# The recurrence of a state-space mixer from twenty steps to eighteen, with four pieces per chunk in separate steps, beside the projections of a decoder layer

## The chip, the core and the metric

The kernel runs on one core of a Trainium2 chip. The metric is the device time of one execution in microseconds (us). The engines are named as the profile names them: PE (TensorE, matrix products and transposes), DVE (VectorE), ACT (ScalarE), POOL (GpSimd) and SP (SyncE, which issues most loads).

## The reference

One decoder layer over 2048 tokens of width 1024, in float32. Its first part, in which the change lies, is a norm, one input projection, and two groups of heads side by side; the second group is the Mamba-2 recurrence in chunks of 128 tokens (12 heads of width 64, 4 groups of B and C, state 128):

```python
h = rmsnorm(x, mix_norm_w)
proj = h @ w_in                       # u (256) | z (768) | x, B, C (768 + 512 + 512) | dt (12)
y_s5 = s5_mixer(proj[..., :256], ...) # the diagonal group
# the recurrence (ssd_mixer): xs, bmat, cmat = silu(causal convolution of width 4)
xdt  = x * dt[..., None]
lmat = exp(where(causal, a_cs[l] - a_cs[s], -inf))        # decay in a chunk
cb   = einsum('bclgn,bcsgn->bcgls', cm, bm)
y_diag = einsum('bcgls,bcghls,bcsghp->bclghp', cb, lmat, xdt)
states = einsum('bclgn,bcghl,bclghp->bcghpn', bm, exp(a_cs[-1] - a_cs), xdt)
def step(carry, inp):                                     # over the 16 chunks
    st, dec = inp
    return carry * dec + st, carry
y = y_diag + einsum(cm, prev, exp(a_cs)) + x * d_skip
y_ssd = rmsnorm(y * silu(z), norm_w)
x = x + concatenate([y_s5, y_ssd]) @ w_out
```

Cross-attention into 256 memory tokens, a gated MLP with a convolution of width 3 and a last norm follow; the change does not touch them.

## The kernel before

Products run as three matmuls on pairs of a rounded value and its rest (`mm3`, L124 to L129): high by high, high by rest, rest by high. So each operand is split (`halves`): ACT writes the rounded half (L102 for weights, L105 for the normed input h), DVE the rest (L103, L106).

The mixer stage (`MixerIn.run`) takes the 2048 tokens in four blocks b of 512, each block in two halves pr of six heads. A block has 22 projections: two of u for the diagonal group, and in each half three of z, three of x, then B, C, B, C. Each projection (`proj`) is two parts of twelve matmuls 128x512; after each part it calls `k.step()`. The outputs of x, B and C go through the width-4 convolution (`conv`): the accumulation bank is read by ACT (L312, L315), the three taps are DVE's (L317), ACT takes the tanh (L319), and DVE's L320 writes the result. The last projection of each half is the second C. Between its last matmul and its L320 lies this whole sequence.

`k.step()` advances three lists of generators by one yield each: fg (the recurrence), bg (the norm of later tokens, the sum of squares `ssq`, the preparation of the memory) and xg (`s5_setup`, the diagonal group's setup, a separate stream that is appended at block 0, half 1; its table operations for POOL are L775 to L783 and its sums of products on DVE L699 to L701). When a half's projections have been issued, its recurrence `ssd(b, pr)` is put on fg and its steps lie between the parts of the projections that follow: those of half 0 in the twenty parts of half 1, those of half 1 in two steps at the next block's start and then in that block's u projections and half 0. At a block's start the eight inputs h of the next block are split with high priority, and their buffers come free when the last projection of the old block has read them. `k.drain()` issues at once what is left at a half's end.

The recurrence has these pieces for each chunk c:

- `decay(c)`: six exponentials on ACT (L407) in a tile of a ring of four that `fetch_L` filled earlier, by a DMA of POOL's queue (L391) and a masking on POOL (L392).
- `stage_in(c)`: three transposes of x (L419) that DVE scales by dt (L421) and by the decay (L422), and two of B (L425) that ACT copies (L427).
- `stage_cb(c)`: two products of B and C (L434), multiplied by the decay on DVE (L438, twice).
- `stage_y(c)`: the products with the old state (L447), the new state (L453) and the chunk itself (L461), with DVE's L449, L455, L456 and L462.
- `stage_out(c)`: three transposes (L470), then DVE's L473 and L474 for each.

After chunk 3 come the squares (ACT's L500, L503, DVE's L504), the scaling by the norm's weight (L505) and three output DMAs on ACT's queue (L506). When half 1 has ended, `ssq` is put on bg: four small matmuls (L517) of the summed squares `sqa`, two steps later.

Before the change the recurrence has twenty yields: `decay(0)`; then `head(0)`, which is `stage_in`, `stage_cb`, the next fetch and the next decay in one step; then for each chunk an empty step, `stage_y(c)`, an empty step, and `head(c+1)` with `stage_out(c-1)` in one step; then `stage_out(3)` and the squares.

A list scheduler orders each engine's queue from the order of issue and the priorities; the engines then work their queues in order and wait for each other by semaphores. Accumulation banks come from one pool of eight (`ps`), the recurrence's small tiles from a pool of fourteen (`u`).

Of the kernel before, what the change touches and what calls it, by code (L numbers as in the profile page):

```python
# [177 lines left out]
class MixerIn:  # L178
# [216 lines left out]
    def ssd(self, b, pr, dd, xs, Bs, Cs, zs, sqacc):  # L395
# [6 lines left out]
        def decay(c):  # L402

            L = Ls[c] = self.L.pop((b, pr, c))
            for hh in range(6):
                h = c * 12 + pr * 6 + hh
                S.activation(L[:, hh, :], L[:, hh, :], AF.Exp, bias=dd["nacs"][:, h:h + 1])  # L407
# [7 lines left out]
        def stage_in(c):  # L415
            cs = slice(c * 128, c * 128 + 128)
            px = k.ps()
            for i in range(3):
                TE.transpose(px[:, i * 128:i * 128 + 128], xs[i][:, cs], k.ident)  # L419
            xdt, xdd = self.u(), self.u()  # L420
            V.tensor_tensor(r6(xdt), r6(px[:, 0:384]), v6(dd["dt"], c), op=ALU.mult)  # L421
            V.tensor_tensor(r6(xdd), r6(xdt), Ls[c][:, :, 127:128].to_broadcast([P, 6, 64]), op=ALU.mult)  # L422
            pB = k.ps()
            for i in range(2):
                TE.transpose(pB[:, i * 128:i * 128 + 128], Bs[i][:, cs], k.ident)  # L425
            Bt = self.u(256)
            S.activation(Bt, pB[:, 0:256], AF.Copy)  # L427
            st[c] = [xdt, xdd, Bt]

        def stage_cb(c):  # L430
            cs = slice(c * 128, c * 128 + 128)
            pc = k.ps()
            for i in range(2):
                TE.matmul(pc[:, i * 128:i * 128 + 128], Bs[i][:, cs], Cs[i][:, cs], start=True, stop=True)  # L434
            M = [self.u() for _ in range(2)]
            for i in range(2):
                m3 = M[i].rearrange("p (h l) -> p h l", h=3)
                V.tensor_tensor(m3, Ls[c][:, i * 3:i * 3 + 3, :], pc[:, i * 128:i * 128 + 128].rearrange("p (h l) -> p h l", h=1).to_broadcast([P, 3, P]), op=ALU.mult)  # L438
            st[c].append(M)

        def stage_y(c):
            cs = slice(c * 128, c * 128 + 128)
            xdt, xdd, Bt, M = st[c]
            po = k.ps()
            for i in range(2):
                o = slice(i * 192, i * 192 + 192)
                TE.matmul(po[:, o], Cs[i][:, cs], self.prev[pr][:, o], start=True, stop=True)  # L447
            yo = self.u()
            V.tensor_tensor(r6(yo), r6(po[:, 0:384]), v6(dd["E"], c), op=ALU.mult)  # L449
            pS = k.ps()  # L450
            for i in range(2):
                o = slice(i * 192, i * 192 + 192)
                TE.matmul(pS[:, o], Bt[:, i * 128:i * 128 + 128], xdd[:, o], start=True, stop=True)  # L453
            np_ = self.u()
            V.tensor_tensor(r6(np_), r6(self.prev[pr]), v6(dd["cd"], c), op=ALU.mult)  # L455
            V.tensor_tensor(np_, pS[:, 0:384], np_, op=ALU.add)  # L456
            self.prev[pr] = np_
            pd = k.ps()
            for h in range(6):
                o = slice(h * 64, h * 64 + 64)  # L460
                TE.matmul(pd[:, o], M[h // 3][:, (h % 3) * 128:(h % 3) * 128 + 128], xdt[:, o], start=True, stop=True)  # L461
            V.tensor_tensor(yo, pd[:, 0:384], yo, op=ALU.add)  # L462
            st[c] = yo

        def stage_out(c):
            cs = slice(c * 128, c * 128 + 128)
            yo = st.pop(c)
            py = k.ps()
            for i in range(3):
                TE.transpose(py[:, i * 128:i * 128 + 128], yo[:, i * 128:i * 128 + 128], k.ident)  # L470
            for i in range(3):
                j = pr * 3 + i
                V.scalar_tensor_tensor(gt[i][:, cs], xs[i][:, cs], self.D[:, j:j + 1], py[:, i * 128:i * 128 + 128], op0=ALU.mult, op1=ALU.add)  # L473
                V.tensor_tensor(gt[i][:, cs], gt[i][:, cs], zs[j][:, cs], op=ALU.mult)  # L474
        def head(c):
            stage_in(c)
            stage_cb(c)
            n = pr * 4 + c + 3
            if n < 8:
                self.fetch_L(b, n // 4, n % 4)  # L480
            if c < 3:
                decay(c + 1)
        head(0)
        yield
        for c in range(4):
            yield
            stage_y(c)
            yield
            yield
            if c < 3:  # L490
                head(c + 1)
            if c:
                stage_out(c - 1)
            yield
        stage_out(3)
        yield
        for i in range(3):
# [1112 lines left out]
```

## Time and profile before

| what | us |
|---|---|
| three runs | 2756.7, 2758.6, 2751.95 |
| their median | 2756.7 |
| profiled execution | 2759.75 |
| its span | 2757.3 |
| PE busy | 2645.7 (96% of the span) |
| DVE busy | 2152.6 (78%) |
| ACT busy | 1326.6 (48%) |
| POOL busy | 495.9 (18%) |
| mean clock that PE was granted | 0.979 |

Durations below are from the one profiled execution, whose time lies 2.45 us over its span and 3.05 us over the median. In rows of a timeline the columns are start, duration, engine, line, operation, output and inputs, shape and count, and in brackets the idle time before it with what ended it. A matmul's duration covers its passage through the array, and matmuls overlap; the distance of starts tells their rate.

### The profile page before, as it was taken

Reading aid. Unit: us, or ns where it says so; the run is one execution under the profiler, and the core shown is the slowest. Engines: PE = TensorE matmul, PEld = TensorE weight load, DVE = VectorE, ACT = ScalarE, POOL = GpSimd, SP = SyncE. Lnnn points to the kernel's source line nnn. Section 1 sums busy time; section 2 is a strip of 40 time slices with the busy share of each in tenths; the row PEclk is TensorE's granted clock in tenths of the full one; section 3 lists DMA queues with packets and bytes.
Section 4 is the critical chain, followed back from the end, with each engine's and each line's share of the span. In section 5 each row is a group of like instructions: output and inputs, shape, how many; then the busy total and the mean of one; then the engine's idle time right before and its main releaser. Section 6 shows DMA issues by size and latency. Waiting matters only on the chain. (4 is left out here: it accounts for less than half of the span.)

```text
span 2757.3 us, 38540 instructions
## 1 busy us (share of the span) xinstructions
PE 2645.7 (96%) x12636; PEld 2199.3 (80%) x12636; DVE 2152.6 (78%) x4015; ACT 1326.6 (48%) x2657; POOL 495.9 (18%) x807
## 2 busy tenths in 40 slices
PE   8989988979999999999999999999999999999988
PEld 6768767857898788888888888887888888888876
DVE  8687788877887754878779788888887877677776
ACT  4654544435555612688745455445443444433333
POOL 1111144542002210110221222211211111000000
PEclk9989989979999999999999999999999999999999
DMA  6455333333259692645665343425322217887886
GB/s 197 154 174 156 123 126 108 117 114 111 92 180 296 236 331 102 230 153 206 210 233 196 116 133 111 133 85 168 103 74 92 84 62 235 287 291 244 261 267 202
DMA packets 241536, 468.22 MB, mean 170 GB/s; under 512 B 30008, under 2 KB 72056, under 8 KB 241336
## 3 DMA queue, kind: packets, MB, share of 16 engines
q1 hardware_dynamic: 182312, 341.38, 36.9%
q0 software_dynamic: 30416, 105.50, 11.8%
q10 hardware_dynamic: 28608, 18.88, 2.2%
q8 instruction: 100, 1.64, 0.2%
q14 instruction: 100, 0.82, 0.1%
HBM read 350.67 MB, written 114.39 MB: 169 GB/s over the span
## 5 line engine op out<-in xcount | busy, mean ns | idle before, releaser
L127 PE MATMUL ps<-H,W 128*128 128x512 f32 x952 | 370.7, 389 | 0.0
L128 PE MATMUL ps<-H,W 128*128 128x512 f32 x952 | 370.5, 389 | 0.2 <-DVE H L103 0.2
L129 PE MATMUL ps<-H,W 128*128 128x512 f32 x952 | 370.5, 389 | 0.1
L127 PE MATMUL ps<-h,w 128*128 128x512 f32 (+1 forms) x736 | 301.2, 409 | 2.5 <-DVE h L106 2.1
L128 PE MATMUL ps<-h,w 128*128 128x512 f32 (+1 forms) x736 | 291.4, 396 | 3.2 <-DVE h L106 3.2
L129 PE MATMUL ps<-h,w 128*128 128x512 f32 (+1 forms) x736 | 290.8, 395 | 2.7 <-DVE w L103 2.7
L127 PE MATMUL ps<-Q,A 128*128 128x512 f32 x704 | 275.8, 392 | 1.2 <-ACT A L102 0.8
L129 PE MATMUL ps<-Q,A 128*128 128x512 f32 x704 | 274.4, 390 | 0.0
L128 PE MATMUL ps<-Q,A 128*128 128x512 f32 x704 | 274.0, 389 | 0.0
L102 ACT ACTIVATE W<-S 128x512 fp32r<-128x512 f32 x191 | 118.9, 630 | 284.5 <-DVE S L1364 141.7
L102 ACT ACTIVATE w<-r 128x512 fp32r<-128x512 f32 x224 | 139.7, 628 | 229.3 <-PE ps L128 161.2
L103 DVE TENSOR_TENSOR w<-r,w 128x512 fp32r<-128x512 f32 x224 | 164.6, 738 | 76.4 <-ACT w L102 75.4
L128 PEld LDWEIGHTS ps<-H,W 128*128 128x128 f32 x952 | 178.7, 188 | 37.7 <-DVE H L103 0.8
L129 PEld LDWEIGHTS ps<-H,W 128*128 128x128 f32 x952 | 178.7, 188 | 37.5 <-DVE W L103 0.5
L127 PEld LDWEIGHTS ps<-H,W 128*128 128x128 f32 x952 | 178.7, 188 | 37.0
L128 PEld LDWEIGHTS ps<-h,w 128*128 128x128 f32 x736 | 142.6, 194 | 33.1 <-DVE h L106 7.2
L129 PEld LDWEIGHTS ps<-h,w 128*128 128x128 f32 x736 | 142.2, 193 | 33.2 <-DVE w L103 3.8
L127 PEld LDWEIGHTS ps<-h,w 128*128 128x128 f32 x736 | 142.6, 194 | 30.3 <-DVE h L106 2.3
L129 PEld LDWEIGHTS ps<-Q,A 128*128 128x128 f32 x704 | 132.1, 188 | 28.6 <-DVE A L103 0.8
L127 PEld LDWEIGHTS ps<-Q,A 128*128 128x128 f32 x704 | 132.2, 188 | 28.5 <-ACT A L102 1.0
L128 PEld LDWEIGHTS ps<-Q,A 128*128 128x128 f32 x704 | 132.2, 188 | 26.7
L102 ACT ACTIVATE A<-F 128x512 fp32r<-128x512 f32 (+1 forms) x146 | 89.0, 631 | 123.5 <-PE ps L128 80.8
(489 smaller groups left out, 6336.5 us busy)
## 6 DMA issues: line engine op xcount, KB each, us to landing
A<-actd SPq DMA_DIRECT2D x192, 256.0 KB, 3.9
r<-in_w_in SPq DMA_DIRECT2D x176, 256.0 KB, 2.9
R<-in_w_up SPq DMA_DIRECT2D x176, 256.0 KB, 2.8
R<-in_w_down SPq DMA_DIRECT2D x132, 256.0 KB, 4.3
actd<-U POOLq DMA_DIRECT2D x88, 256.0 KB, 3.1
A<-actd SPq DMA_DIRECT2D x96, 192.0 KB, 3.8
R<-h3Cd SPq DMA_DIRECT2D x56, 256.0 KB, 3.5
L<-acsd POOLq DMA_DIRECT2D x32, 384.0 KB, 4.6
```

What stands on the lines that cost most here:

```text
L102: self.S.activation(hi, src, AF.Copy)
L103: self.V.tensor_tensor(lo, src, hi.bitcast(F32), op=ALU.subtract)
L127: self.TE.matmul(out, lh, rh, start=first and i == 0, stop=False)
L128: self.TE.matmul(out, lh, rl, start=False, stop=False)
L129: self.TE.matmul(out, ll, rh, start=False, stop=last and i == n - 1)
```

## The change

The pieces of the recurrence are the same, and so is their work. They are dealt to steps anew: `stage_in(0)` has a step of its own, `stage_cb(c)` with the fetch and the decay of the next chunk a step, `stage_in(c+1)` a step, `stage_y(c)` a step, and from chunk 1 on `stage_out(c-1)` a step. There are no empty steps and eighteen yields.

```diff
-        def head(c):
-            stage_in(c)
+        stage_in(0)
+        yield
+        for c in range(4):
             stage_cb(c)
             n = pr * 4 + c + 3
             if n < 8:
                 self.fetch_L(b, n // 4, n % 4)
             if c < 3:
                 decay(c + 1)
-        head(0)
-        yield
-        for c in range(4):
             yield
+            if c < 3:
+                stage_in(c + 1)
+                yield
             stage_y(c)
             yield
-            yield
-            if c < 3:
-                head(c + 1)
             if c:
                 stage_out(c - 1)
-            yield
+                yield
         stage_out(3)
         yield
```

Counted in yields, with the step at which each piece is issued:

| piece | before | after |
|---|---|---|
| in 0, 1, 2, 3 | 2, 6, 10, 14 | 2, 4, 7, 11 |
| cb 0, 1, 2, 3 (with fetch and decay) | 2, 6, 10, 14 | 3, 6, 10, 14 |
| y 0, 1, 2, 3 | 4, 8, 12, 16 | 5, 8, 12, 15 |
| out 0, 1, 2, 3 | 10, 14, 18, 19 | 9, 13, 16, 17 |
| squares, output DMAs | 20 | 18 |

Lines behind the changed part have numbers smaller by two after the change (L504 becomes L502, L701 becomes L699, L742 becomes L740).

PE's queue at the first recurrence, block 0 half 0, whose steps lie in the z projections of half 1 (`t` are the convolutions' results, `ps` accumulation banks). Before:

```order
L419 MATMUL ps<-ident,t 128x128 x3
L425 MATMUL ps<-ident,t 128x128 x2
L434 MATMUL ps<-t 128x128 x2
L127 MATMUL ps<-h,w 128x512
...
L447 MATMUL ps<-u,t 128x192 x2
L453 MATMUL ps<-u 128x192 x2
L461 MATMUL ps<-u 128x64 x6
```

After:

```order
L419 MATMUL ps<-ident,t 128x128 x3
L425 MATMUL ps<-ident,t 128x128 x2
L127 MATMUL ps<-h,w 128x512
...
L434 MATMUL ps<-t 128x128 x2
L127 MATMUL ps<-h,w 128x512
...
L419 MATMUL ps<-ident,t 128x128 x3
L425 MATMUL ps<-ident,t 128x128 x2
L127 MATMUL ps<-h,w 128x512
...
L447 MATMUL ps<-u,t 128x192 x2
L453 MATMUL ps<-u 128x192 x2
L461 MATMUL ps<-u 128x64 x6
```

Each "..." is the rest of a projection's part; before, the one gap holds twenty-four matmuls 128x512, after, each of the three holds twelve. `cb(0)` (L434) stands twelve matmuls later, and chunk 1's transposes have moved ahead of `y(0)`.

PE's queue from the last projections of block 0 to the first of block 1 (L152 are transposes of the norm of later tokens, L338 the dt projection of block 1, which reads the new h). Before:

```order
L419 MATMUL ps<-ident,t 128x128 x3
L425 MATMUL ps<-ident,t 128x128
L434 MATMUL ps<-t 128x128
L152 MATMUL ps<-ident,raw 128x128 x4
L127 MATMUL ps<-h,w 128x512
...
L425 MATMUL ps<-ident,t 128x128
...
L453 MATMUL ps<-u 128x192 x2
L434 MATMUL ps<-t 128x128
L447 MATMUL ps<-u,t 128x192
L461 MATMUL ps<-u 128x64 x6
L338 MATMUL ps<-h,wd 24x512
```

After:

```order
L425 MATMUL ps<-ident,t 128x128
L152 MATMUL ps<-ident,raw 128x128 x4
L127 MATMUL ps<-h,w 128x512
...
L434 MATMUL ps<-t 128x128
...
L419 MATMUL ps<-ident,t 128x128 x3
L425 MATMUL ps<-ident,t 128x128
L338 MATMUL ps<-h,wd 24x512
...
L434 MATMUL ps<-t 128x128
L447 MATMUL ps<-u,t 128x192
L453 MATMUL ps<-u 128x192 x2
L461 MATMUL ps<-u 128x64 x6
```

The second product of `cb(0)` (the second L434, which reads the last convolution's result) stood ahead of the sixteen L338; now the L338 and twelve matmuls of the second u projection stand ahead of it. Ahead of it are also both parts of the first u projection, before and after.

DVE's queue at the same place, around the last two splits of h (L106). Before:

```order
L106 SCALAR_TENSOR_TENSOR h<-r,gains,h 128x512
L473 SCALAR_TENSOR_TENSOR t<-t,D,ps 128x128
L311 COPY t<-halo 128x3
...
L421 TENSOR_TENSOR u<-ps,dt 128x384
L134 TENSOR_SCALAR ss<-ss 128x1
L422 TENSOR_TENSOR u<-u,L 128x384
L504 TENSOR_TENSOR sqa<-sqa,t 128x512
```

After:

```order
L106 SCALAR_TENSOR_TENSOR h<-r,gains,h 128x512
L143 TENSOR_SCALAR raw<-raw,ss 128x1024
L106 SCALAR_TENSOR_TENSOR h<-r,gains,h 128x512
L502 TENSOR_TENSOR sqa<-sqa,t 128x512
L311 COPY t<-halo 128x3
L719 TENSOR_TENSOR td<-ident,dsk 16x64
L502 TENSOR_TENSOR sqa<-sqa,t 128x512
L421 TENSOR_TENSOR u<-ps,dt 128x384
L422 TENSOR_TENSOR u<-u,L 128x384
```

The tail of the old recurrence (four L473 and L474, then the squares) stood behind the last split; most of it now stands ahead of or among the splits, and the squares follow directly.

## The prediction

> **What bounds the kernel now.** I read the page's table of engines first, then busy time by stretches of the span, then TensorE's (PE's) waits, then the timeline around the longest ones. The chain of waits covers only the last few microseconds and says nothing here.
>
> ```profile
> PE 2645.7 (96%) x12636; PEld 2199.3 (80%) x12636; DVE 2152.6 (78%) x4015; ACT 1326.6 (48%) x2657; POOL 495.9 (18%) x807
> ...
> PEclk9989989979999999999999999999999999999999
> ```
>
> PE is the bound, and it falls below full clock only in the first 700 us, the mixer stage. By stretches (columns: window, length, busy time of each engine with instructions, granted clock, DMA share, GB/s):
>
> ```profile
> 110.00:175.00 65.00, 65.00 (x364) 55.98 (x363) 49.86 (x107) 35.60 (x75) 10.95 (x14) 0.99 0.45 144
> 1000.00:2000.00 1000.00, 996.55 (x4582) 828.06 (x4581) 796.24 (x1336) 539.50 (x1139) 188.54 (x317) 1.00 0.48 161
> 99.00:111.00 12.00, 7.40 (x26) 5.84 (x25) 7.59 (x14) 4.43 (x9) 1.14 (x2) 0.72 0.52 177
> 177.00:208.00 31.00, 19.76 (x72) 13.78 (x71) 23.94 (x52) 15.36 (x27) 1.67 (x2) 0.72 0.54 179
> 302.00:316.00 14.00, 9.44 (x33) 7.24 (x32) 10.38 (x20) 4.20 (x8) 2.17 (x3) 0.63 0.31 104
> 376.00:403.00 27.00, 16.02 (x57) 10.34 (x56) 21.59 (x42) 8.81 (x17) 13.98 (x25) 0.62 0.42 137
> 462.00:489.00 27.00, 18.46 (x68) 14.32 (x67) 26.93 (x39) 13.51 (x29) 25.07 (x30) 0.81 0.37 121
> 562.00:605.00 43.00, 25.59 (x77) 15.61 (x77) 34.21 (x51) 16.43 (x28) 21.12 (x24) 0.64 0.41 135
> 672.00:682.00 10.00, 5.88 (x23) 4.64 (x22) 7.38 (x17) 7.96 (x16) 1.56 (x1) 0.83 0.56 170
> sum 164.00, PE 102.55 PEld 71.78 DVE 132.03 ACT 70.70 POOL 66.72; mean PE 14.65 PEld 10.25 DVE 18.86 ACT 10.10 POOL 9.53
> ```
>
> The first two rows are PE with nothing to gain. The seven others are the ends of the mixer's halves, which I call A1 to A7, and hold nearly all that a reordering can win: 164.00 - 102.55 = 61.45 us idle, plus clock. An upper bound of a boundary's cost is its idle time plus (1 - clock) x length: 8.0, 19.9, 9.7, 21.2, 13.7, 32.9 and 5.8, together 111 us (idle time at half clock counts twice in it). What PE waits for there (engine, line and releaser, total us, times, longest):
>
> ```profile
> PE ps L434 <- DVE t L320: 22.7, 7, 5.6
> PE ps L517 <- DVE sqa L504: 10.2, 2, 6.1
> ...
> PE ps L434 <- ACT raw L283: 3.2, 1, 3.2
> PE ps L152 <- DVE t L473: 2.4, 1, 2.4
> ```
>
> The largest is chunk 0's `cb` (L434), which needs the convolutions of the last projections (L320); the change moves just that.
>
> **The change, part by part.** No arithmetic comes or goes: the same transposes, products, exponentials and DMAs are issued. So nothing is gained or lost outside the boundaries, where PE was full in the rows above and each displaced item has matmuls around it.
>
> *cb(0) one step later, A1 and A3.*
>
> ```profile
> 96.24 0.48 PE L127 MATMUL ps<-h,w 128*128 128x512 f32 x1
> ...
> 98.87 0.40 PE L129 MATMUL ps<-h,w 128*128 128x512 f32 x1
> 99.10 0.49 PE L419 MATMUL ps<-ident,t 128*128 128x128 f32 x3
> ...
> 99.65 0.39 PE L434 MATMUL ps<-t 128*128 128x128 f32 x2
> 104.63 0.80 PE L434 MATMUL ps<-t 128*128 128x128 f32 x2 [4.60 <-DVE t L320]
> ```
> ```profile
> 100.00:104.00 4.00, 0.03 (x1) 0.00 (x0) 2.71 (x6) 2.84 (x6) 0.55 (x1) 0.98 0.57 176
> 104.00:110.00 6.00, 5.37 (x14) 4.30 (x15) 3.74 (x7) 0.11 (x1) 0.59 (x1) 0.50 0.45 153
> ```
>
> The twelve matmuls of one step run from 96.24 to 99.10: 2.86 us at full clock. After the change they stand between the transposes of chunk 0 and `cb(0)`, so the 4.60 us wait becomes about 1.7. The clock was still 0.98 in the wait's first four microseconds and 0.50 in the six after it; 5.37 us of half clock are worth 2.7. If the shorter wait keeps the clock, A1 gains 2.86 + 2.7 = 5.6; if not, 2.9. I take 5.5, nearer the row of 100 to 104, where the clock stood longer than 1.7 us of idling. A3:
>
> ```profile
> 303.93 0.33 PE L425 MATMUL ps<-ident,t 128*128 128x128 f32 x1 [1.54 <-DVE t L320]
> ...
> 308.44 0.80 PE L434 MATMUL ps<-t 128*128 128x128 f32 x2 [2.54 <-DVE t L320]
> ```
> ```profile
> 305.00:310.00 5.00, 2.45 (x9) 1.44 (x8) 4.64 (x9) 1.60 (x3) 0.00 (x0) 0.53 0.33 117
> ```
>
> Here PE has 24 matmuls ahead of the second `cb(0)` before and 32 after, as well as the transposes of chunk 1: 8 x 0.24 = 1.9 us and 0.55 (99.10 to 99.65 above), so the 2.54 us wait goes and the 1.54 us one stays. Gain between 2.5 and 8 (idle and clock); taken 4.5.
>
> *The start of a block, A2, A4, A6.* Here DVE is the bound between the last convolutions and `cb(0)`:
>
> ```profile
> 170.38 0.69 DVE L320 SCALAR_TENSOR_TENSOR t<-t 128x512 f32<-128x512 f32 x1 [3.82 <-ACT t L319]
> ...
> 182.47 0.76 DVE L106 SCALAR_TENSOR_TENSOR h<-r,gains,h 128x512 fp32r<-128x512 f32 x1
> ...
> 188.91 0.57 DVE L421 TENSOR_TENSOR u<-ps,dt 128x384 f32<-128x384 f32 x1
> ...
> 189.99 0.68 DVE L504 TENSOR_TENSOR sqa<-sqa,t 128x512 f32<-128x512 f32 x1
> ...
> 193.06 0.69 DVE L701 TENSOR_TENSOR t<-t 128x512 f32<-128x512 f32 x1
> ...
> 198.24 0.69 DVE L320 SCALAR_TENSOR_TENSOR t<-t 128x512 f32<-128x512 f32 x1 [0.70 <-ACT t L319]
> ```
> ```profile
> 198.99 0.79 PE L434 MATMUL ps<-t 128*128 128x128 f32 x2 [5.57 <-DVE t L320]
> ...
> 203.01 5.40 PE L338 MATMUL ps<-h,wd 128*24 128x512 f32 x16
> 211.01 0.60 PE L742 MATMUL ps<-ident,t 128*128 128x128 f32 x4
> ```
>
> DVE has 28.6 us of nearly unbroken work from 170.38 to the last L320. Counted by the new order with the durations of such rows, 28.5 us stand ahead of that L320, so `cb(0)` is still free only at about 199.5. What changes is what PE has done by then: the sixteen L338 (5.40 at half clock) and the first twelve matmuls of the next projection (from 208.4 to 211.0) now stand ahead of the wait. Behind it remain `cb(0)`'s second half and `y(0)`'s products, 4.0 us as from 198.99 to 203.01, and at 203.5 PE is where it was at 211.0: gain 7.5, from which 0.5 goes for the next block's h, whose last split (L106, at 182.47) stands behind some 3 us more DVE rows; PE used most of those h only behind its own wait of 3.24 us. Taken 7 for A2, with bounds of -7 (the late h leaves no cover and costs as worked out with the slower rival) and 13 (idle and clock both). A4 has the same pattern, a wait of two pieces and clock 0.62: taken 8, bounds -7 to 13. A6 has the largest cost, but its decays wait for GpSimd:
>
> ```profile
> 555.79 0.69 ACT L407 ACTIVATE L<-L,nacs 128x128 f32<-128x128 f32 x2 [7.08 <-POOL L L392]
> ```
> ```profile
> 555.73 0.61 POOL L775 TENSOR_TENSOR tab<-fCa,fb 128x256 f32<-128x256 f32 x1
> ...
> 557.47 1.18 POOL L777 TENSOR_TENSOR tab<-tab,wk 128x256 f32<-128x256 f32 x1
> ```
>
> In the new order four table operations (L775 to L782, 0.6 to 1.2 us each, about 3.5) pass ahead of this fetch on GpSimd's queue, and ScalarE's convolutions stand behind the decay. Gain like A4's, 8 to 10, less about 3: taken 6, bounds -10 to 15.
>
> *The tail (out 2, out 3, squares, three output DMAs) one or two steps earlier.* It is a fixed cost on ScalarE and DVE that moves from behind the h splits to among them; A2's 0.5 above is its price. It also starts the sum of squares (L517) earlier:
>
> ```profile
> 456.22 6.55 DVE L320 SCALAR_TENSOR_TENSOR t<-t 128x512 f32<-128x512 f32 x1 [2.01 <-ACT t L319]
> ```
> ```profile
> 478.48 1.84 PE L517 MATMUL ps<-one,sqa 128*128 128x1 f32 x8 [6.12 <-DVE sqa L504]
> ```
>
> In A5 the wait has another root: DVE itself is stretched, one L320 from about 0.7 to 6.55 us, while GpSimd is busy 25.07 of 27 us with tables, which the change does not touch. `sqa` and L517 move by the same two steps, so I take 0, bounds -3 to +6. In A7 GpSimd is quiet, and of the 4.12 us idle (10.00 - 5.88) about half goes: 2, bounds 0 to 5. The output DMAs (L506) are 12 in all, go to ScalarE's queue and are read only after the mixer: 0. The fetches on GpSimd keep their order against each other: 0, apart from A6.
>
> The sum: 5.5 + 7 + 4.5 + 8 + 0 + 6 + 2 = 33 us. The profiled execution took 2759.75 (span 2757.3 and 2.45 around it), which is 3.05 over the median of 2756.7; 2759.75 - 33 - 3 = **2724**.
>
> **Rivals.**
>
> *The wait only moves (no change).* For it: DVE and not PE's order sets when L434 is free at A2, A4 and A6, and work done ahead of the wait helps only if h comes in time. Then A1 and A3 gain what their matmuls cover, 2.9 and 2.5, and the rest nothing: 2751. Against it: the L338 and u1 matmuls need no result of the recurrence.
>
> *The tail and chunk 1's inputs stand in front of h (slower).* At each block start L504 twice (0.68 each), three S5 rows (L699 to L701, as the 0.69 at 193.06) and chunk 1's two scalings (L421, and L422 like it, 0.57 each) may run before the last h: 4.6 us, three times, 13.8; GpSimd's 3.5 at A6; and the transposes of chunk 1 hold two more accumulation banks while DVE is behind, as L152 waited 2.4 us for one: 3 x 2.4 = 7. That is 24; less 5.4 for A1 and A3, 2775. It decides if h comes more than about 6 us later than now (gain 7.5 lost and 3.5 more at each start): then PE idles in front of the new cover. Against it: I count 3.
>
> *The clock stays full at all boundaries (much faster).* After the change no wait I foresee at A1, A3 and A4 exceeds 3 us, and if the clock drops only after one long wait, all of (1 - clock) x length there goes: 3.4 + 5.2 + 10.3, and half at A2 and A6, 4.3 + 7.7, so 31, on top of the covered idle time, 2.9 + 2.5 + 3 x 6.5 = 25: 56 us, 2701. Against it is A3: its longest wait is 2.54 us, and the clock fell to 0.53 all the same, after three waits close together.
> [...]
>
> **How the numbers follow.** A change under 0.3% (8.3 us) can't be told from none. Chances: forecast (2705 to 2742) 0.62; clock rival 0.14; wait only moves 0.15; slower rival 0.09. Of the wait-only case two thirds lie within 8.3 us and a third gains a little more; of the slower rival a fifth ends within. So faster 0.81, same 0.12, slower 0.07. The terms' bounds together reach from 22 us slower to 66 faster; all low or all high at once is unlikely, so the range runs from the clock rival's 2701 to 2752, just past the wait-only case. The likeliest case alone: 2705 to 2742.
>
> **What would show it.** Right: at A1 one wait of L434 of about 1.7 us and clock near 1 between 104 and 110; at the block starts the L338 rows ahead of the second L434; the L434 total of 22.7 below 15, and PE's idle time before 700 us lower by some 20. Wrong: new long waits for L106 or for a bank at 177 to 190 and 376 to 390 (slower rival); L434 waits as long as now at 199 (wait only moves); A6 longer than 43 us (GpSimd's order). Anything beyond 700 us that moves more than 2 us I have not foreseen.

## The result, and the profile after

| | median us | range | runs |
|---|---|---|---|
| before | 2757.65 | 2751.95 to 2760.48 | 4 |
| after | 2718.45 | 2715.65 to 2722.86 | 4 |

The ratio after to before is 0.9862, with a 95% interval of 0.9841 to 0.9883: 39 us less. Forecast was 2724, 33 us below the median of 2756.7 that was known then. The profile after, its engines and the granted clock:

```profile
PE 2631.4 (97%) x12636; PEld 2191.7 (81%) x12636; DVE 2144.2 (79%) x4015; ACT 1323.2 (49%) x2657; POOL 492.3 (18%) x807
...
PEclk9999998999999999999999999999999999999999
```

The instructions are the same in number. The span went from 2757.3 to 2717.5 us, and nearly all of it in the first 700 us. Those stretches of the kernel before and, second, after:

```profile
0.00:700.00 700.00, 628.81 (x3081) 515.40 (x3081) 559.72 (x1329) 345.97 (x703) 195.60 (x277) 0.93 0.42 137
```
```profile
0.00:700.00 700.00, 649.81 (x3272) 537.30 (x3273) 581.08 (x1386) 360.28 (x744) 196.50 (x283) 0.97 0.45 142
```

PE idles 21 us less (71.2 to 50.2) and runs more of the rest at full clock (mean 0.97 against 0.93). The same boundaries after the change, A1, A2, A3, A4, A5, A6, A7 in this order, then three places that were full before:

```profile
97.00:109.00 12.00, 10.23 (x52) 8.39 (x52) 10.25 (x18) 5.88 (x13) 1.14 (x2) 1.00 0.56 184
170.00:186.00 16.00, 11.55 (x51) 9.66 (x50) 14.05 (x29) 12.66 (x23) 0.94 (x1) 0.79 0.83 266
280.00:296.00 16.00, 16.00 (x87) 13.55 (x86) 16.00 (x33) 7.18 (x14) 3.66 (x4) 1.00 0.46 143
350.00:372.00 22.00, 17.35 (x76) 10.51 (x75) 21.84 (x35) 12.91 (x24) 17.18 (x28) 1.00 0.64 193
425.00:450.00 25.00, 17.08 (x63) 13.38 (x62) 24.93 (x30) 12.09 (x25) 23.40 (x29) 0.80 0.35 116
535.00:578.00 43.00, 34.89 (x145) 24.68 (x144) 35.03 (x55) 20.27 (x35) 17.72 (x21) 0.84 0.47 148
628.00:645.00 17.00, 11.78 (x43) 9.52 (x42) 14.06 (x33) 14.01 (x32) 1.05 (x1) 0.80 0.41 131
```
```profile
149.00:161.00 12.00, 9.47 (x45) 8.23 (x45) 10.63 (x25) 3.46 (x7) 1.93 (x3) 0.86 0.47 143
460.00:476.00 16.00, 13.79 (x60) 11.04 (x59) 11.65 (x22) 6.80 (x14) 0.61 (x1) 0.89 0.33 107
515.00:526.00 11.00, 8.01 (x37) 6.88 (x36) 10.96 (x20) 2.74 (x5) 10.21 (x13) 0.84 0.35 119
```

A1 keeps its clock, A3 is simply gone (16.00 of 16.00 busy), A4 keeps full clock through 4.65 us of idling, A5 and A7 are about as they were. The last three rows are new losses. PE's waits of the mixer stage after the change:

```profile
PE ps L515 <- DVE sqa L502: 11.1, 2, 5.9
PE ps L128 <- DVE h L106: 7.9, 10, 2.3
PE ps L461 <- DVE u L438: 5.7, 3, 3.0
PE ps L152 <- DVE raw L143: 4.4, 1, 4.4
PE ps L434 <- DVE t L320: 3.8, 2, 2.0
```

The wait for `cb(0)` (L434) fell from 22.7 us to 3.8. The one for h rose from 3.0 to 7.9, and L461, the chunk's own products in `y(c)`, now waits for DVE's masking of `cb` (L438), which it hardly did before. At A2 the sixteen L338 stand in front of `cb(0)`; the same line's answer after and, second, before (duration in ns as minimum, median and maximum, then first and last start):

```profile
L338 PE MATMUL ps<-h,wd x16: 389/397/479, 188.5 to 192.3; 128*24 128x512 f32 x8, 128*12 128x512 f32 x8
```
```profile
L338 PE MATMUL ps<-h,wd x16: 390/456/667, 203.0 to 208.0; 128*24 128x512 f32 x8, 128*12 128x512 f32 x8
```

They start 14.5 us earlier and run at full clock (1.00 from 188.5 to 192.7). No wait for L320 is left at A2; PE's one wait there is now for the norm of later tokens:

```profile
178.88 1.09 PE L152 MATMUL ps<-ident,raw 128*128 128x128 f32 x4 [4.45 <-DVE raw L143]
```

The projections follow each other in the same order in every version, so the start of the same projection's first matmul (L127) can be compared between traces. The differences, after less before, part by part (negative is time won; "to its last C" is the stretch that leads to the half's last C projection, and so to its end):

| stretch | after less before, us |
|---|---|
| start to A1 | -1.8 |
| A1 | -5.1 |
| b0 half 1, to its last C (near 155) | +5.3 |
| A2 | -11.3 |
| to A3 | +0.9 |
| A3 | -9.5 |
| A4 | -10.0 |
| A5 | -1.5 |
| behind A5, near 469 | +4.5 |
| b2 half 1, to its last C | +4.6 |
| A6 | -13.2 |
| A7 and behind it | +0.9 |
| the rest of the kernel | -3.6 |

Each trace is of one execution, and such a part scatters. Four of the versions below (the one with only `cb(0)` and `y(0)` moved, the same without GpSimd's tables, and the two with the tables elsewhere) have the same order of operations on PE, DVE, ACT and GpSimd up to the end of A4. Still A1 is 4.0 to 5.7 us shorter in them than before, A2 10.5 to 13.0 and A4 6.3 to 10.8. So a difference of less than some 5 us in one part is not shown by one pair of traces alone.

### The profile page after: what moved, and what is told of

Read it like the earlier page. It is cut to its first block, busy times and chain, and to the rows that moved or that the text cites. A ratio compares the mean times of both kernels' runs of the same rounds, so it can differ in the third digit from the quotient of the medians.

```text
span 2717.5 us, 38526 instructions
## 1 busy us (share of the span) xinstructions
PE 2631.4 (97%) x12636; PEld 2191.7 (81%) x12636; DVE 2144.2 (79%) x4015; ACT 1323.2 (49%) x2657; POOL 492.3 (18%) x807
## 5 line engine op out<-in xcount | busy, mean ns | idle before, releaser
L127 PE MATMUL ps<-H,W 128*128 128x512 f32 x952 | 371.2, 390 | 0.0
L127 PE MATMUL ps<-h,w 128*128 128x512 f32 (+1 forms) x736 | 304.2, 413 | 4.1 <-ACT h L105 2.6
L127 PE MATMUL ps<-Q,A 128*128 128x512 f32 x704 | 276.1, 392 | 0.6 <-ACT A L102 0.6
L103 DVE TENSOR_TENSOR w<-r,w 128x512 fp32r<-128x512 f32 x224 | 159.3, 714 | 69.1 <-ACT w L102 67.7
L127 PEld LDWEIGHTS ps<-H,W 128*128 128x128 f32 x952 | 178.8, 188 | 36.9
L128 PEld LDWEIGHTS ps<-h,w 128*128 128x128 f32 x736 | 142.3, 193 | 39.0 <-DVE h L106 14.5
L127 PEld LDWEIGHTS ps<-h,w 128*128 128x128 f32 x736 | 141.9, 193 | 30.0 <-ACT h L105 2.9
L127 PEld LDWEIGHTS ps<-Q,A 128*128 128x128 f32 x704 | 132.3, 188 | 27.3 <-ACT A L102 0.8
```

The lines of the kernel that those rows point to most:

```text
L103: self.V.tensor_tensor(lo, src, hi.bitcast(F32), op=ALU.subtract)
L127: self.TE.matmul(out, lh, rh, start=first and i == 0, stop=False)
L128: self.TE.matmul(out, lh, rl, start=False, stop=False)
```

## The experiments

Steps are counted in yields as in the table of the change. Each ratio is to the kernel before on the same chip. The diffs are written short: `cb0_fetch_decay()` stands for `stage_cb(0)` with the fetch and the decay of chunk 1.

**cb(0) alone one step later** (from the kernel before):

```diff
-        head(0)            # in 0, cb 0, fetch, decay 1
-        yield
+        stage_in(0)
+        yield
+        cb0_fetch_decay()  # in the place of the empty step
         yield
         stage_y(0)         # step 4, as before
```

> Only the split of chunk 0: stage_in(0) in step 2, cb(0) with fetch and decay in step 3 (an empty step before), everything else on the steps of the kernel before. Theory (cover by cb(0) alone at half ends, by chunk 1's early inputs and the moved wait at block starts): A1 gains its 5.3 us as in the changed kernel, A3 4 to 8, the block starts A2, A4, A6 at most 3 each because the second L434 still stands ahead of the sixteen L338; no new waits of L461 near 155 and 520. Sum 12 to 20 less than before, about 2740. Rival (the shorter tail is what gains): within 3 us of before, 2757. Rival (cb(0)'s place is everything): all of it, 2718.

Measured 2751.55 us, ratio 0.9989 (0.9976 to 1.0002): no change that can be told from none. Of the three expectations only the rival that had the shorter tail as the gain comes near in time; its reason is tested further down. The trace says what happened. Windows of A1 and A3, the waits at A3, and the one at A1:

```profile
97.00:109.00 12.00, 9.55 (x56) 8.25 (x54) 10.04 (x18) 5.51 (x11) 1.14 (x2) 1.00 0.53 172
294.00:310.00 16.00, 11.69 (x42) 9.19 (x41) 10.97 (x22) 5.39 (x11) 2.18 (x3) 0.68 0.28 91
```
```profile
296.22 0.33 PE L425 MATMUL ps<-ident,t 128*128 128x128 f32 x1 [1.54 <-DVE t L320]
297.02 1.65 PE L453 MATMUL ps<-u 128*128 128x192 f32 x4 [0.47 <-ACT u L427]
300.73 0.79 PE L434 MATMUL ps<-t 128*128 128x128 f32 x2 [2.06 <-DVE t L320]
```
```profile
103.30 0.49 PE L434 MATMUL ps<-t 128*128 128x128 f32 x2 [2.45 <-DVE t L320]
```

The last row is A1's wait. A1 gains its 5.0 us. A3 is as before, with the same three waits, and so are A2, A4 and A6 (-1.2, -0.2, +1.4). There the queue had put `cb(0)`'s second product among the products of `y(0)` already, whatever step had issued it; that it does so because DVE frees the product so late is likely, but was not shown. So a later `cb(0)` moves nothing there.

**cb(0) back with in(0)** (from the changed kernel):

```diff
         stage_in(0)
-        yield
         stage_cb(0) ...
         yield
+        yield
         stage_in(1)
```

> The changed kernel with cb(0) back in the step of stage_in(0) and an empty step behind it; chunk 1 to 3's inputs early and all else as in the changed kernel. Theory: A1 loses its 5.3 us (wait of L434 of about 4.5 us, clock 0.5 after it), A3 loses 2 to 6, the block starts keep their gain, since the sixteen L338 and the first matmuls of u1 still stand ahead of the second L434. Sum 7 to 12 over the changed kernel, about 2728. Rival (cb(0)'s place is everything): all of the gain lost, 2757.

Measured 2724.28 us, ratio 0.9889 (0.9872 to 0.9906), 6 us over the changed kernel. PE's wait at A1 is back:

```profile
103.32 0.80 PE L434 MATMUL ps<-t 128*128 128x128 f32 x2 [4.75 <-DVE t L320]
```

A1 gains nothing against before (+0.6), while A3 keeps -9.5, A2 -10.8 and A4 -10.7. The theory had A3 lose 2 to 6; it lost nothing. With the run before this leaves two candidates for everything but A1: `y(0)`, which stands at step 5 in the changed kernel and at 4 before, and the early inputs of chunks 1 to 3.

**y(0) alone one step later** (from the kernel before):

```diff
         head(0)
         yield
         yield
+        yield
         stage_y(0)         # step 5
         yield
-        yield
         head(1)            # step 6, as before
```

> The kernel before with one thing moved: y(0) one step later (step 5, as in the changed kernel), cb(0) still in the step of in(0), chunks 1 to 3 and the tail on the steps of before. Theory (y(0)'s step is the lever, since the queue keeps the second product of cb(0) just ahead of y(0), and DVE frees it late): A1 gains nothing, A2, A3, A4 and A6 gain 9 to 13 each as in the changed kernel (sum 40 to 44), and the new waits near C10 of blocks 0 and 2 (4.8 and 5.1) do not come: 2712 to 2718. Rival (chunk 1's early inputs are needed as cover, or free DVE's queue): 10 to 20 gained, about 2740. Rival (nothing alone): 2755.

Measured 2719.54 us, ratio 0.9862 (0.9838 to 0.9885): one step for one piece gives the whole change's ratio. Windows of A1 and A3, and the wait:

```profile
97.00:109.00 12.00, 7.46 (x26) 5.93 (x25) 7.64 (x14) 4.22 (x9) 1.14 (x2) 0.72 0.50 170
290.00:306.00 16.00, 15.62 (x83) 12.74 (x82) 14.95 (x29) 8.26 (x18) 2.96 (x5) 1.00 0.44 141
```
```profile
PE ps L434 <- DVE t L320: 11.6, 4, 4.7
```

A1 is as before (7.46 busy of 12.00, clock 0.72), and A2, A3, A4 and A6 give 8.8, 8.0, 7.7 and 10.0. The three new waits of the changed kernel do not come. The time lies just above the theory's 2712 to 2718, as the four parts win 34.5 us and not 40 to 44.

**Both, and nothing else** (from the kernel before, cb(0) at step 3 and y(0) at step 5):

```diff
-        head(0)
+        stage_in(0)
+        yield
+        cb0_fetch_decay()
         yield
         yield
         stage_y(0)
         yield
-        yield
         head(1)
```

> The kernel before with cb(0) at step 3 and y(0) at step 5 and nothing else moved: both of the places of the changed kernel's chunk 0, with the inputs of chunks 1 to 3, the outputs and the tail as before. Theory (the two moves add): the 5.0 of A1 and the 40 to 44 of the block starts and A3, and none of the changed kernel's losses (4.8, 4.5 and 5.1 us): 2705 to 2712, 6 to 13 less than the changed kernel. Rival (early inputs needed): 2730 to 2740.

Measured 2709.49 us (2708.17 to 2712.44), ratio 0.9825 (0.9804 to 0.9846). Its slowest run is below the fastest of the changed kernel (2715.65). It is the fastest version here that computes everything; PE is busy for 654.75 us of the first 700.

Against before, A1 is -5.7, A2 -12.9, A3 -7.4, A4 -10.8, A6 -10.7, and of the changed kernel's three losses (the stretches around the new waits: +4.8 near 155, +4.5 behind A5, +5.1 near 520) none comes. The 49 us are more than the 3 and 39 of the two moves alone, but the intervals of the three ratios do not tell this from a plain sum. So the rest of the change (early inputs, `y(3)`, outputs and tail earlier, no empty steps) costs some 9 us; the next runs look for the part that does.

**The early inputs, on top of the last version** (in 1, 2, 3 at steps 4, 7, 11):

```diff
+            stage_in(c + 1)   # two or three steps ahead of cb(c + 1)
             yield
             stage_y(c)
             ...
-            stage_in(c + 1)
             stage_cb(c + 1)
```

> The version with only cb(0) (step 3) and y(0) (step 5) moved, plus the inputs of chunks 1, 2 and 3 two or three steps early (4, 7, 11) as in the changed kernel; y(3), the outputs and the tail stay on the steps of before (16; 10, 14, 18, 19, 20). Theory (the early inputs are no cover that is needed, and their transposes and DVE rows are what delays L438 near 155 and 520): the changed kernel's losses come back, 2716 to 2720. Rival (the losses are from y(3) and the outputs one or two steps earlier): as without the early inputs, 2707 to 2712. Rival (early inputs are useful cover): below 2705.

Measured 2727.49 us median, with the profiled execution at 2717.77 the fastest of four; ratio 0.9888 (0.9863 to 0.9913). The early inputs are no cover that is needed; they cost 10 us by the profiled executions (2717.77 against 2708.17) and 18 by the medians; the other three runs, 9 to 12 us slower, left no trace. In the trace the loss behind A5 and the one near 520 come back (+4.9 and +5.6 against the version without them), though A5 itself gains 6.5. The one near 155 does not come (0.0); A2, A4 and A7 lose 6.4, 3.3 and 4.2.

**y(3) two steps behind cb(3)** (from the changed kernel):

```diff
             stage_cb(3)
             yield
+            yield
             stage_y(3)
```

> The changed kernel with one empty step between cb(3) and y(3), as before the change; the tail follows one step later. Theory (the two new waits of PE for DVE's L438 near 155 and 520, 2.5 and 3.0 us and about 4.6 us each with the clock, come from y(3) being one step behind cb(3) instead of two): both waits go, and 9 us with them, 2709 to 2712. Rival (DVE is late there by itself): the waits move to another line in the same place and the time stays at 2718. Rival (the later tail costs what is won): 2715 to 2725, with the loss at the block starts.

Measured 2717.65 us, ratio 0.9862 (0.9846 to 0.9879): the time of the changed kernel. Waits, and the row near 524:

```profile
PE ps L515 <- DVE sqa L502: 21.2, 3, 11.0
```
```profile
524.61 1.55 PE L461 MATMUL ps<-u 128*128 128x64 f32 x12 [2.54 <-DVE u L438]
```

The wait near 155 is gone (that stretch +0.3 instead of +4.8), but the one near 520 stays (+4.7), and what is won is lost elsewhere: the wait for the summed squares, where halves end, doubles from 11.1 to 21.2 us. So the wait near 155 comes from `y(3)` standing one step behind `cb(3)`; the one near 520 does not come from that alone.

**Outputs behind cb in the same step** (from the changed kernel: out 0 and out 1 at steps 10 and 14, behind cb 2 and cb 3):

```diff
             stage_cb(c) ...
+            if c > 1:
+                stage_out(c - 2)
             yield
             ...
-            if c:
-                stage_out(c - 1)
-                yield
+            if c == 1 or c == 2:
+                yield
+        stage_out(2)
+        yield
         stage_out(3)
```

> The changed kernel with out(c-1) issued behind cb(c+1) in the same step instead of a step ahead of it (out 0 at 10, out 1 at 14; out 2, out 3 and the squares unchanged). Theory (the new waits for L438 near 155 and 520 come from the L473 and L474 of out(1) standing ahead of cb(3)'s L438 in DVE's queue): both waits go, 8 to 10 us less than the changed kernel, 2709. Rival (the convolution rows L317 ahead of L438 are enough, or GpSimd's tables beside them at 520): one or both stay, 2713 to 2718.

Measured 2724.89 us, ratio 0.9878 (0.9855 to 0.9900): a miss. The stretch near 520 costs 11.5 against before, the one near 155 still 4.7. The two places differ. Near 155 the wait for L438 is gone, as the theory had it: DVE runs L438 at 153.03, ahead of the output's L473. But the next output's transposes (L470, at 164.76) now wait 2.51 us for DVE's L462, and the loss stays. Near 520 DVE also runs L438 ahead of L473, and PE's wait for it, 7.49 us at 529.07, is longer than ever; there the outputs' rows are not the cause.

**The tail late** (from the changed kernel, two empty steps ahead of out 2):

```diff
             stage_y(3)
             yield
+            yield
+            yield
             stage_out(2)
```

> The changed kernel with two empty steps ahead of out(2), so that out 2, out 3, the squares and the DMAs stand on the steps of before (18, 19, 20). Theory (the tail's place is of no weight): within 5 us of the changed kernel, 2713 to 2724, A1 and A3 as in the changed kernel, the wait for h at the block starts shorter by 2 to 4 us, and the wait for sqa (L515) at A5 as long. Rival (the tail's two steps earlier give the gain, since h and the convolutions are then alone): 15 to 25 us lost, about 2740, at the block starts alone.

Measured 2717.41 us, ratio 0.9867 (0.9845 to 0.9890): the tail's place has no weight for the whole, as the prediction's price of 0.5 had it. The waits for h are 2.1 us shorter in all, as expected. The wait of the squares' product at A5 is not as long but longer, 7.32 us against 5.91; A5 is 3.5 us worse and the stretch behind it 3.9 better. The run with `y(3)` two steps behind `cb(3)` has the same exchange (3.6 and 4.0). A2 gains 3 more and A4 2 less than in the changed kernel.

**Without GpSimd's tables** (the changed kernel, and then the version with cb(0) and y(0) alone):

```diff
-        G.tensor_tensor(tab[:, 0], a_(ca), b_(cb), op=ALU.mult)
-        ...                        # six products and sums per table
+        G.memset(tab, 0.0)
```

> The changed kernel without the products of GpSimd's tables (the two L775, L776 products and sums and so on are left out, a zero fill stands in their place; the table's DMA stays), so the diagonal group's values are not computed. Theory (DVE's rows at A5, near 520 and at A6 are stretched while GpSimd reads for the tables): A5 loses its wait of 5.9 us for sqa and the half clock behind it, 8 to 12 us; the wait near 520, 5; A6 3 to 8. Sum 16 to 25 less than the changed kernel, about 2698. Rival (the waits are DVE's own backlog): within 5 us of the changed kernel.

> The version with only cb(0) and y(0) moved, without the products of GpSimd's tables (a zero fill in their place, so the diagonal group's values are not computed). It bounds what moving the tables out of DVE's way can bring. Theory (the tables' cost at A5, A6 and A7 adds to the recurrence's steps): 30 to 39 us less than with the tables, 2670 to 2680. Rival (part of the 39 us measured on the changed kernel were its own losses near 520 and behind A5, which this version does not have): 2685 to 2695.

Measured 2679.12 us (ratio 0.9713, 0.9692 to 0.9734) and 2681.84 us (0.9728, 0.9710 to 0.9745). For the first the theory's sum was too small (39 us less than the changed kernel, against 16 to 25): A5 and the place near 520 are as named, A6 gains 14.9 instead of 3 to 8, and A7 was not named; the second lies between its two expectations, 28 us below the same version with tables. Without tables the changed kernel is 2.7 us ahead of the other, within the intervals, with them 9 behind, so what the rest of the change costs goes with the tables. Waits of the first:

```profile
PE ps L461 <- DVE u L438: 2.9, 4, 2.2
...
PE ps L515 <- DVE sqa L502: 0.3, 1, 0.3
```

The wait for the summed squares, 11.1 us, is gone, and with it most of A5's and A7's cost; the stretch near 520 is as before the change (+0.2), the one near 155 is not (+4.5). So 155 is `y(3)`'s step: all four traces that keep it one step behind `cb(3)`, with the first two outputs where the changed kernel has them, show the wait for L438 (0.65 to 2.53 us), and no trace with `y(3)` two steps behind loses more than 0.3 us there. And 520 needs two things, the tables and the early inputs: each of the six traces with both loses 4.7 to 11.5 us there, every other at most 0.2. DVE's operations from 420 to 600 us (busy us, mean ns), the version with tables and, second, without:

```profile
L320 DVE SCALAR_TENSOR_TENSOR t<-t 128x512 f32<-128x512 f32 x13 | 13.5, 1036 | 3.6 <-ACT t L319 3.6
L106 DVE SCALAR_TENSOR_TENSOR h<-r,gains,h 128x512 fp32r<-128x512 f32 x8 | 9.6, 1201 | 0.0
...
L438 DVE TENSOR_TENSOR u<-L,ps 128x384 f32<-128x384 f32 x16 | 8.1, 546 | 0.6 <-PE ps L434 0.6
```
```profile
L320 DVE SCALAR_TENSOR_TENSOR t<-t 128x512 f32<-128x512 f32 x16 | 11.4, 713 | 2.2 <-ACT t L319 2.2
...
L438 DVE TENSOR_TENSOR u<-L,ps 128x384 f32<-128x384 f32 x16 | 8.1, 550 | 0.6 <-PE ps L434 0.6
L106 DVE SCALAR_TENSOR_TENSOR h<-r,gains,h 128x512 fp32r<-128x512 f32 x8 | 6.0, 750 | 0.0
```

L320 and L106, whose inputs lie all in SBUF, take 1036 and 1201 ns on average in the stretch with tables and 713 and 750 without (the two windows hold slightly different pieces of the program, thirteen and sixteen L320). L438, which reads one input from an accumulation bank, takes 546 and 550. In the changed kernel's own trace, from 340 to 640 us, four L320 ran at the same time as a table operation and took 0.85 to 1.81 us, against 0.67 to 0.89 for the sixteen others; two pairs of L438 that did (at 484.53 and 520.11) took 1.00 us each, and the pairs that did not 1.01 to 1.02. Whether the place of the inputs makes this difference was not shown.

The stretched rows are not the only way in which the tables cost time. They also stand in GpSimd's own queue ahead of the fetches for the decay. ScalarE at A6, with tables and, second, without:

```profile
520.07 0.70 ACT L407 ACTIVATE L<-L,nacs 128x128 f32<-128x128 f32 x2 [9.49 <-POOL L L392]
```
```profile
503.15 0.69 ACT L407 ACTIVATE L<-L,nacs 128x128 f32<-128x128 f32 x2 [1.63 <-POOL L L392]
```

A6 is where leaving the tables out wins most (17 us more in the version with two pieces moved). How much of that is DVE's rows and how much GpSimd's queue, these runs do not separate.

**The tables elsewhere** (from the version with cb(0) and y(0) alone; nothing left out): 38 empty steps ahead of them, or half a table per step in the middle of each half only (and, for what is left, behind the last half).

```diff
+    for _ in range(38):          # the first
+        yield
     for g in range(16):
+        while not k.mid:         # the second: set from z 2 to the last x projection
+            yield
         G.tensor_tensor(tab[:, 0], ...)
```

> The version with only cb(0) and y(0) moved, and 38 empty steps ahead of GpSimd's tables, so that they start in the last block's first z projections (near 585) instead of near 420 and end in the memory's projections; nothing is left out. Theory (the tables cost where they meet a half's end; in the last block they meet only A7): A5 and A6 gain as without tables (10 and 15), A7 and the end of the mixer lose 5 to 10: 2690 to 2697. Rival (tables cost the same wherever DVE is loaded): 2705 to 2715. Rival (the tables come too late for the diagonal group's stage, which reads the first near 765): over 2715.

> The version with only cb(0) and y(0) moved, and GpSimd's tables held back so that half a table is issued per step only in the third z projection and the three x projections of a half (eight of twenty steps), over blocks 2 and 3; nothing is left out. Theory (tables cost where they meet the convolutions of B and C, the h splits and the sum of squares at a half's end): A5, A6 and A7 as without tables, with up to 10 us left, 2682 to 2695. Rival (tables beside DVE cost wherever they run, as when they were put 38 steps later): 2705 to 2718.

Measured 2717.94 us (0.9860, 0.9835 to 0.9884) and 2718.32 us (0.9860, 0.9838 to 0.9882): 8 to 9 us worse than where the tables were (no run of either is as fast as the slowest there, 2712.44; the intervals of the ratios overlap a little). Against that version A5 and A6 gain 12.2 and 14.0 with the later tables (10.6 and 8.2 with the spread ones), A7 loses 10.1 (3.0), the last half 7.1 (10.4). A4 is 4.5 worse in both, though no table stands there and the queues up to its end are the same: that is scatter. From the second part of the last projection on, another 12.7 us are lost in both (span less its start: 2717.2 - 703.75 and 2719.3 - 705.81, against 2706.4 - 705.67). The end of the mixer with the spread tables and, second, without the move:

```profile
695.00:735.00 40.00, 30.50 (x181) 27.38 (x181) 31.57 (x68) 19.06 (x38) 2.51 (x4) 0.87 0.36 109
```
```profile
695.00:735.00 40.00, 37.22 (x263) 34.48 (x262) 34.33 (x75) 21.88 (x44) 1.22 (x1) 1.00 0.37 115
```

The theory that tables cost only where they meet a half's end fell: what was won at A5 and A6 was lost elsewhere. The time of the first also fits its rival of tables that come too late for the diagonal group, but that did not happen: the last table is sent off at 710 us, and the first is read at 780. Nor is the loss at the end of the mixer a row stretched by tables. With the spread tables GpSimd is busy for 2.51 of these 40 us, and PE's longest wait there is 5.64 us for the split of a weight (L103); what pushed this work back was not separated.

## Why the prediction came out right, point by point

*The time.* 2724 forecast, 2718.45 measured, within the likeliest case's 2705 to 2742; its sign and size were right. Its terms against the traces:

| term | forecast | measured | |
|---|---|---|---|
| A1 | 5.5 | 5.1 | right in its working, with luck in the clock |
| A2, with the half ahead of it | 7 | 6.0 | 11.3 won, 5.3 lost ahead of it |
| A3, with the half ahead of it | 4.5 | 8.6 | 9.5 won, 0.9 lost; too small, and for the wrong reason |
| A4 | 8 | 10.0 | |
| A5, with the loss behind it | 0 | -3.0 | 1.5 won, 4.5 lost |
| A6, with the half ahead of it | 6 | 8.6 | 13.2 won, 4.6 lost |
| A7 | 2 | -0.9 | |
| not foreseen (start, rest) | 0 | 5.4 | 1.8 and 3.6 |

That the sum came so near is in part luck. The seven boundaries gave about 50 us where 33 were forecast, and 15 were lost between them where nothing was forecast. Of the 5.4, the start's share is no gain of the change: the trace of before is late there by 1.6 us, against all others but one.

*cb(0) as the lever.* At A1 the step was right: 4.60 us of waiting were to become 1.7 and the clock was to hold. The trace has

```profile
102.75 0.49 PE L434 MATMUL ps<-t 128*128 128x128 f32 x2 [1.77 <-DVE t L320]
```

and clock 1.00 in the window. That the clock held was luck. In eight of the traces with `cb(0)` in its later step this one wait is 1.77 to 2.45 us long; in four of them the clock held, in four it fell, and then A1 gained 3.4 to 4.1 us instead of 5.5 (the last section has the waits). At A3 the step failed. It put the gain down to `cb(0)` passing eight more matmuls and chunk 1's transposes; a later `cb(0)` alone gave nothing there, and with `cb(0)` at its old step A3 gained its 9.5 all the same. The 1.54 us wait of L425, which was to stay, went too. The lever is `y(0)`, one step later: the queue holds the second L434 among the products of `y(0)`, and one step more lets another part of a projection run before both.

*The block starts.* That the L338 and the first matmuls of the second u projection run ahead of `cb(0)` was right, and it is what their starts at 188.5 show. The prediction read it off the order correctly and did not ask which of the moved pieces allows it; `y(0)` alone gives 8.8, 7.7 and 10.0 there. The price at A6 for GpSimd's order, about 3 us, did not show as a longer wait: the exponentials wait 4.18 us for their mask, against 7.08 before. The output DMAs that were put at 0 are 24 in all, three for each half, and not 12.

*"Nothing is gained or lost outside the boundaries."* This step failed, and it is the one that matters: the term was put at nothing because each displaced piece had matmuls around it. Three new waits came where PE had been full:

```profile
155.57 1.08 PE L461 MATMUL ps<-u 128*128 128x64 f32 x6 [2.53 <-DVE u L438]
```
```profile
469.72 0.49 PE L434 MATMUL ps<-t 128*128 128x128 f32 x2 [1.99 <-DVE t L320]
```
```profile
520.70 2.28 PE L461 MATMUL ps<-u 128*128 128x64 f32 x12 [2.99 <-DVE u L438]
```

With the clock behind them (0.86, 0.89 and 0.84 in the windows of these three places) the stretches around them lost 4.8, 4.5 and 5.1 us (5.3 and 4.6 for the whole halves with the first and the third, in the table above). The table of steps had shown the first: `y(3)` at 15 instead of 16, one step behind `cb(3)`. It was read as a gain in length and not as a lost spare step. The third needs the early inputs and the tables together. The second has its companion in A5, where DVE's L320 takes 1.79 and 1.81 us beside the tables (at 434.39 and 447.63): in the two runs with a later tail the stretch behind A5 loses 0.5 and 0.6 and A5 itself is as much worse, so what is lost at the two together stays at 2.5 to 3. Which piece shifts it was not separated.

*A5 and the tables.* Taking A5's cost as DVE stretched by GpSimd fits the runs (without tables the wait for the summed squares is 0.3 us in all instead of 11.1), and so does that the change hardly touches it.

*The rivals.* The slower one had h more than 6 us late; the waits for h rose by 4.9 us in all, over ten waits. That the wait only moves did not come: L434's fell by 18.9 us. The clock rival came true in part: the clock was 1.00 at A1, A3 and A4, but 0.79 at A2 and 0.84 at A6, and the three new waits took part of the sum back.

## What to carry to other kernels

When a change deals the same pieces to new steps, look in the order for the piece that holds the waiting product in its place, and move that one alone: here one piece by one step gave all of the gain, and two pieces gave 9 us more than the whole redistribution. A spare step between a product and its consumer is cover for the engine between them; counting it as an empty step loses it. And where DVE is the bound at a boundary, see which GpSimd work runs beside it before the order is tuned: leaving it out was worth 39 us on the changed kernel and 28 on the version with two pieces moved, while the two ways of moving it that were run won nothing. Last, a part's difference between two single executions counts only beyond the scatter of equal queues, here up to 4.5 us.

## What the runs showed of the hardware

In these runs the length of a short wait did not tell whether the clock fell. At A1 the clock held with waits of 1.77, 1.88, 1.88 and 2.45 us in four executions (matmuls 128x512 start 0.23 us apart behind the wait) and fell with waits of 1.79, 1.84, 1.87 and 1.93 us in four others (0.43 us apart). At A4 of the changed kernel it held with a wait of 2.03 us; the waits of 2.53 us at 155.57 and 1.99 us at 469.72 were followed by half clock.

In the traces of before and after, each of the 25 changes of the granted clock lies on a grid of 3.41 us, and the grid lies differently against the start of the span: an edge is at 11.71 us before and at 12.74 us after. Here are stretches of this grid from the changed kernel: that of the wait of 2.53 us and the one behind it, that of the wait of 2.03 us, and that of the wait of 1.99 us and the one behind it.

```profile
152.69:156.10 3.41, 0.88 (x8) 0.58 (x6) 3.41 (x11) 2.30 (x4) 0.00 (x0) 1.00 0.51 154
156.10:159.51 3.41, 3.41 (x17) 3.22 (x16) 3.41 (x8) 0.60 (x1) 1.37 (x2) 0.50 0.53 145
364.31:367.73 3.42, 1.52 (x7) 0.45 (x5) 3.42 (x7) 1.63 (x3) 3.24 (x5) 1.00 0.48 159
466.71:470.13 3.42, 1.44 (x9) 1.13 (x8) 3.42 (x7) 1.91 (x4) 0.00 (x0) 1.00 0.36 106
470.13:473.54 3.41, 3.41 (x10) 2.63 (x10) 1.67 (x4) 0.00 (x0) 0.61 (x1) 0.50 0.38 124
```

With PE busy for 0.88 and 1.44 us of a stretch the next one was at 0.50; with 1.52 us it stayed at 1.00. Counted over these two traces from 30 us on, half clock followed each of the 19 full-clock stretches in which PE was busy for less than 43%, 5 of the 33 with 43 to 70%, and 1 of the 1483 with more. The wait of 1.77 us at A1 of the changed kernel was divided by the edge at 101.49; PE was busy for 2.91 us of the stretch before that edge and for 2.15 us of the one behind it, and the clock was 1.00 in both and in the next.
